# Attention columns of the first projection: six plain groups against three pairs of groups with two seven-product steps each

## The chip, the cores and the metric

The program runs on 1 core of one Trainium2 chip. The metric is the device time of one execution in microseconds (us), lower is better. The kernel before has a median of 1235.88 us over 3 runs (1235.82 to 1235.96).

The core has five engines with queues of their own: TensorE (PE, matmuls; its weight loads are listed apart as PEld), VectorE (DVE), ScalarE (ACT), GpSimd (POOL), and SyncE (SP), which here issues the loads from device memory. PE multiplies a moving operand by a stationary one and adds into PSUM, eight banks of 128 partitions by 512 fp32 columns; everything else lies in SBUF.

## What is computed

One decoder layer for 256 tokens and width 2048, in fp32, cut to what matters here:

```python
h = rms_norm(x, mix_norm_g[i])
z = h @ w_in[i]                                    # 2048 x 7184
mq, mk, mv, mo, mi, mf, fq, fk, fv, ff = jnp.split(z, split_points, axis=-1)
...                                                # mLSTM heads (A), forgetting attention (B) -> ha, hb
x = x + jnp.concatenate([ha, hb], axis=-1) @ w_out[i]
h = rms_norm(x, ffn_norm_g[i])
u = h @ w_up[i]
...                                                # causal conv, GELU, gate, w_down, and a gated last projection
```

The columns 4096 to 7183 of `w_in` (the gates mi, mf, ff and the attention inputs fq, fk, fv, 3088 columns) are the "FOX columns". They are computed first, then mq, mk, mv, mo.

## The kernel before

Weights arrive in fp32. Each weight block is split in two parts, hi (a cast to the PE's reduced fp32 form, on ACT) and lo (raw minus hi, on DVE); the left side is split in the same way once. One exact product then is three matmuls that add into one PSUM bank: left-hi by hi, left-hi by lo, left-lo by hi (lines 308, 309, 310 in this part of the program). The 256 tokens are two tiles of 128 rows (t = 0, 1); the inner dimension of 2048 is 16 K tiles of 128.

`token_group` (line 289) makes a group of n columns out of blocks. A block holds two K tiles of n columns (up to 1024 elements per partition), and takes 2 x 2 x 3 = 12 matmuls. The FOX columns are seven groups, of 512, 432 (five times) and 416 columns. In the first group x itself is also loaded, normed by a gain and transposed (lines 148, 149, 157) into `hT`, the left side. A group adds into two banks (one for each t) of the tag "mm", which has four; the tag "aux" has the other four, for transposes and for the side work. At a group's end ACT evacuates each bank, scaled by `rstd_mix` (line 751).

`run_stream` (line 250) runs all blocks of this part: the load of block i+3 is issued while block i is multiplied, into three load buffers (raw0 to raw2) in turn; up to three blocks are split ahead, into four pairs of buffers (hi0/lo0 to hi3/lo3), so a split waits until the block four back is multiplied. Between blocks it pulls two steps of the side work (head norms, gate arithmetic, attention heads, mLSTM heads), written as generators. A scheduler then sets the order on each engine's queue from its own estimate of when operands are there; the order in the source is its starting point.

Later, in the up projection, the kernel has the scheme that the change brings here: groups of four banks, with some pairs of K tiles done in seven products (lines 1336 to 1393). There 512 columns are a half, and the splits may run four units ahead.

Of the kernel before, what the change touches and what calls it, by code (L numbers as in the profile page):

```python
# [9 lines left out]
F32 = mybir.dt.float32  # L10
F32R = mybir.dt.float32r
AF = mybir.ActivationFunctionType
ALU = mybir.AluOpType
# [17 lines left out]
FOX_WIDTHS = (512, 432, 432, 432, 432, 432, 416)  # L31
# [8 lines left out]
AHEAD_DMA, AHEAD_SPLIT = 3, 3  # L40
# [14 lines left out]
def layer_kernel(  # L55
# [194 lines left out]
    def run_stream(blocks, pulls, ramp=False):  # L250

        nb = len(blocks)
        raws, parts = {}, {}
        split = 0
        for i in range(-AHEAD_DMA, nb):
            j = i + AHEAD_DMA
            if j < nb:
                src, _, _, load = blocks[j][:4]
                if load is not None:
                    load()  # L260
                kb, n = src.shape[1], src.shape[2]
                raws[j] = wp.tile([P, BLK], F32, tag=f"raw{j % RAW}", name=f"raw{j}", bufs=1)
                nc.sync.dma_start(out=raws[j][:, : kb * n].rearrange("p (k n) -> p k n", k=kb), in_=src)

            ahead = min(AHEAD_SPLIT, 1 + i // 2) if ramp else AHEAD_SPLIT
            while i >= -1 and split < min(nb, i + ahead + 1):
                j, split = split, split + 1
                src, _, prep, _ = blocks[j]
                if prep is not None:
                    prep()  # L270
                kb, n = src.shape[1], src.shape[2]
                w = kb * n
                raw = raws.pop(j)
                hi = wp.tile([P, BLK], F32R, tag=f"hi{j % PARTS}", name=f"hi{j}", bufs=1)
                lo = wp.tile([P, BLK], F32R, tag=f"lo{j % PARTS}", name=f"lo{j}", bufs=1)
                hi, lo = hi[:, :w], lo[:, :w]
                act.copy(hi, raw[:, :w])  # L277
                last["hi"] = traced()
                dve.tensor_sub(lo, raw[:, :w], f32(hi))  # L279
                parts[j] = [v.rearrange("p (k n) -> p k n", k=kb) for v in (hi, lo)]  # L280
            if i >= 0:
                blocks[i][1](*parts.pop(i))
                done[0] += 1
                pull(pulls)
# [4 lines left out]
    def token_group(w, korder, actT, c0, n, finish, tag="mm", prep=None, load=None):  # L289
# [7 lines left out]
        for bi, (k0, kb) in enumerate(starts):  # L297
            def fn(hi, lo, bi=bi, k0=k0):
                if bi == 0:
                    st["b"] = [bank(tag, f"tg{t}") for t in range(NT)]  # L300
                for t in range(NT):
# [9 lines left out]
                    if bi == len(starts) - 1:  # L311
                        finish(t, st["b"][t])
            pair = k0 % 2 == 0
            blocks.append((wsrc(w, k0, kb, c0, n), fn, pair and prep and (lambda k0=k0: prep(k0)) or None,
                           pair and load and (lambda k0=k0: load(k0)) or None))
        return blocks

# [29 lines left out]
    with mixers:  # L347
# [407 lines left out]
        ready_at = {"fq": (lambda: fox_norm("fq", 8),), "fk": (lambda: fox_norm("fk", 0),), "fv": (gate_math, fox_heads)}  # L755
        c0 = C_MI
        for n in FOX_WIDTHS:
            jobs = [j for name, o, w in runs_ if c0 < o + w <= c0 + n for j in ready_at[name]]
            kw = dict(prep=prep_x, load=load_x) if c0 == C_MI else {}
            add(c0, n, after(fox_evac(c0, n), *jobs), **kw)  # L760
            c0 += n
# [42 lines left out]
        for c in range(4):  # L804
            grp = token_group(w_out, kcat, lambda: catT, c * 512, 512, resid(c, ssq2, get_x2T, g_ffn))
            if c == 0:
                src, fn, _, _ = grp[4]
                grp[4] = (src, lambda hi, lo, fn=fn: (pull_all(), fn(hi, lo)), None, None)
            blocks.extend(grp)
        run_stream(blocks, 2, ramp=True)  # L810
# [3 lines left out]
    with tc.tile_pool(name="ffn", bufs=1) as fp:  # L814
# [44 lines left out]

        def sums_of(u, f, t):  # L860

            a11, a12 = u[:, 0, 0:P], u[:, 1, 0:P]
            dve.tensor_sub(f[:, 1::2], u[:, 0].rearrange("p (i c) -> p i c", c=P), u[:, :, P:S])
            dve.tensor_sub(f[:, 0], f[:, 3], a11)
# [170 lines left out]
        def units(blocks):  # L1035
            return [Unit([b[0]], b[1]) for b in blocks]
# [440 lines left out]
```

## Time and profile before

| what | value |
|---|---|
| median of 3 runs | 1235.88 us |
| the profiled execution: its time, its span | 1236.08 us, 1234.2 us |
| PE busy, PE weight loads busy | 1227.8 us (99%), 1035.5 us (84%) |
| DVE busy, ACT busy, POOL busy | 925.0 us (75%), 734.5 us (60%), 185.5 us (15%) |
| matmuls | 5620 |
| HBM read, mean rate | 247.46 MB, 208 GB/s |

The span runs from the first to the last instruction; 1.9 us of the profiled execution lie outside of it. Successive matmuls overlap in the profile (a row of 0.36 us can start every 0.19 us), so a matmul's price is the distance from one start to the next, not its listed duration. In a row of groups, the first number after the bar is the busy time in us, the second the mean duration in ns, and after the second bar stands the engine's idle time just before such instructions, with what ended it.

### The profile page before, as it was taken

What the parts mean: (1) busy time and instruction counts of PE and PEld (TensorE: products, weight loads), DVE (VectorE), ACT (ScalarE), POOL (GpSimd) and SP (SyncE); (2) the same over time, 40 slices, a digit from 0 to 9 for tenths busy, and PEclk for the clock granted to TensorE, in tenths of its full rate; (3) what the DMA queues carried; (4) which work ended last, traced back from release to release, by engine and by line L of the source; (5) the groups of instructions that cost most, each with busy time, mean ns of one, the idle gap of its engine ahead of it and who ended that gap; (6) DMA issues with size and microseconds to landing.
All of it is one profiled execution on the core that took longest, in us unless ns stands there. A gap on an engine that the chain in (4) does not pass through costs nothing.

```text
span 1234.2 us, 16266 instructions
## 1 busy us (share of the span) xinstructions
PE 1227.8 (99%) x5620; PEld 1035.5 (84%) x5620; DVE 925.0 (75%) x1107; ACT 734.5 (60%) x1071; POOL 185.5 (15%) x347
## 2 busy tenths in 40 slices
PE   9999999999999999999999999999999999999998
PEld 7999988888888888888888888888888888888887
DVE  6455566665565589789998898998788998898653
ACT  8565455554554465766676676757666555565542
POOL 2001256513304201011101100110110000050000
PEclk9999999999999999999999999999999999999999
DMA  8766878766567786777687678666897896777560
GB/s 257 195 187 185 226 222 219 208 196 179 171 188 218 222 307 207 242 220 235 211 271 243 184 253 271 223 180 213 245 315 245 305 332 210 258 231 257 176 214 35
DMA packets 139490, 276.35 MB, mean 224 GB/s; under 512 B 14905, under 2 KB 36913, under 8 KB 139281
## 3 DMA queue, kind: packets, MB, share of 16 engines
q1 hardware_dynamic: 127504, 256.87, 66.6%
q0 software_dynamic: 11520, 18.29, 5.2%
q8 instruction: 44, 0.72, 0.2%
q14 instruction: 37, 0.30, 0.1%
q10 hardware_dynamic: 385, 0.16, 0.0%
HBM read 247.46 MB, written 8.93 MB: 208 GB/s over the span
## 4 chain that ended last, share of the span: by engine, by line
PE 99%; DMA 0%; SPq 0%; DVE 0%; ACT 0%; issue 0%; DVEq 0%
PE tg L308 13%; PE tg L309 13%; PE tg L310 13%; PE up L1320 11%; PE up L1321 11%; PE up L1319 11%; PE dnP L1082 1%; PE upP L1319 1%; PE upP L1321 1%; PE upP L1320 1%; PE dnP L1080 1%; PE dnP L1081 1%; PE dn(0, 1)_7898 L1080 1%; PE dn(0, 0)_7894 L1080 1%; PE dn(1, 0)_7902 L1080 1%; PE dn(0, 1)_7898 L1082 1%
## 5 line engine op out<-in xcount | busy, mean ns | idle before, releaser
L279 DVE TENSOR_TENSOR lo<-raw,hi 128x1024 fp32r<-128x1024 f32 (+3 forms) x153 | 177.7, 1162 | 154.3 <-ACT hi L277 153.9
L277 ACT CAST hi<-raw 128x1024 fp32r<-128x1024 f32 (+3 forms) x153 | 153.4, 1003 | 155.3 <-PE tg L310 116.3
L1321 PE MATMUL up<-part,x2T 128*128 128x512 f32 x608 | 236.6, 389 | 0.0
L1320 PE MATMUL up<-part,x2T 128*128 128x512 f32 x608 | 236.5, 389 | 0.0
L1030 ACT CAST part<-raw 128x1024 fp32r<-128x1024 f32 (+1 forms) x147 | 147.1, 1009 | 112.4 <-PE up L1321 34.2
L1032 DVE TENSOR_TENSOR part<-raw,part 128x1024 fp32r<-128x1024 f32 (+1 forms) x141 | 163.2, 1162 | 34.3 <-ACT part L1030 31.7
L1319 PE MATMUL up<-part,x2T 128*128 128x512 f32 x608 | 185.0, 389 | 0.0
L309 PE MATMUL tg<-lo,hT 128*128 128x512 f32 (+2 forms) x480 | 181.5, 378 | 0.0
L308 PE MATMUL tg<-hi,hT 128*128 128x512 f32 (+2 forms) x480 | 180.8, 382 | 0.0
L310 PE MATMUL tg<-hi,hT 128*128 128x512 f32 (+2 forms) x480 | 180.3, 377 | 0.0
L1319 PEld LDWEIGHTS up<-part,x2T 128*128 128x128 f32 x608 | 114.1, 188 | 23.7
L1321 PEld LDWEIGHTS up<-part,x2T 128*128 128x128 f32 x608 | 114.1, 188 | 23.7
L1320 PEld LDWEIGHTS up<-part,x2T 128*128 128x128 f32 x608 | 114.1, 188 | 23.7
L310 PEld LDWEIGHTS tg<-hi,hT 128*128 128x128 f32 x480 | 90.1, 188 | 12.4
L309 PEld LDWEIGHTS tg<-lo,hT 128*128 128x128 f32 x480 | 90.2, 188 | 11.7 <-DVE lo L279 0.3
L308 PEld LDWEIGHTS tg<-hi,hT 128*128 128x128 f32 x480 | 89.7, 188 | 11.8
L195 POOL DMA_DIRECT2D EZ<-Y x66 | 35.1, 539 | 371.7 <-issue 205.1
L1030 ACT CAST part<-u36r 128x1024 fp32r<-128x1024 f32 (+1 forms) x46 | 47.9, 1043 | 33.5 <-PE up L1321 16.2
L1032 DVE TENSOR_TENSOR part<-u36r,part 128x1024 fp32r<-128x1024 f32 (+1 forms) x46 | 55.6, 1208 | 10.0 <-ACT part L1030 5.8
L1032 DVE TENSOR_TENSOR part<-u32r,part 128x1024 fp32r<-128x1024 f32 (+1 forms) x44 | 50.4, 1146 | 12.2 <-ACT part L1030 9.4
L1030 ACT CAST part<-u32r 128x1024 fp32r<-128x1024 f32 (+1 forms) x44 | 43.5, 994 | 21.1 <-PE up L1321 8.9
L310 PE MATMUL tg<-hi,catT 128*128 128x512 f32 x128 | 49.9, 390 | 0.0
(752 smaller groups left out, 2311.8 us busy)
## 6 DMA issues: line engine op xcount, KB each, us to landing
raw<-in_w_up_dram SPq DMA_DIRECT2D x78, 512.0 KB, 5.0
raw<-in_w_in_dram SPq DMA_DIRECT2D x71, 512.0 KB, 4.3
u36r<-in_w_up_dram SPq DMA_DIRECT2D x43, 512.0 KB, 5.0
raw<-in_w_down_dram SPq DMA_DIRECT2D x42, 512.0 KB, 5.9
u32r<-in_w_up_dram SPq DMA_DIRECT2D x34, 512.0 KB, 5.1
raw<-in_w_in_dram SPq DMA_DIRECT2D x40, 432.0 KB, 3.8
raw<-in_w_out_dram SPq DMA_DIRECT2D x32, 512.0 KB, 4.9
xs<-in_w_up_dram SPq DMA_DIRECT2D x21, 512.0 KB, 4.8
```

Of the source, the lines that this page charges most:

```text
L195: (other if other and (4 * a + b) % 3 else pool).dma_start(out=c[32 * b : 32 * b + 32, a::4], in_=y[32 * a : 32 * a + 32, :, b])
L277: act.copy(hi, raw[:, :w])
L279: dve.tensor_sub(lo, raw[:, :w], f32(hi))
L308: pe.matmul(o, ah, hi[:, i, :], start=first, stop=False)
L309: pe.matmul(o, ah, lo[:, i, :], start=False, stop=False)
L310: pe.matmul(o, al, hi[:, i, :], start=False, stop=last)
L1030: act.copy(r32(hi), raw)
L1032: dve.tensor_sub(r32(lo), raw, hi)
L1080: pe.matmul(o, ah, hi, start=first, stop=False)
L1319: pe.matmul(o, ah, hi, start=start, stop=False)
L1320: pe.matmul(o, ah, lo, start=False, stop=False)
L1321: pe.matmul(o, al, hi, start=False, stop=stop)
```

## The change

The FOX columns become one plain group of 512 and three pairs of groups. A pair holds two halves of 430 columns (428 in the last pair) side by side; a block is one K tile of both halves, and the pair adds into four banks, (t, half). Twelve of its 16 K tiles ("p") are plain: 2 x 2 x 3 = 12 matmuls. K tiles 0, 1 ("a") and 2, 3 ("b") are each a 2 x 2 block product (two token tiles, two K tiles, two halves) done by seven products of three matmuls, 21 in place of 24, in four units of 3, 6, 6 and 6 matmuls. Three of the seven add straight into the pair's banks, four go into four banks of their own (P1, P5, P6, P7), shared by a and b. The order of units in a pair is `"pppp" "apapapap" "bpbpbpb" "p"`; the two sets of four banks, "mm" and "aux", change roles from pair to pair, so all eight banks are used.

For the sums of left parts (`make_S`, `sums_of`) DVE and ACT make two tiles S_h in the first group. For the sums of weights DVE adds halves of the loaded tiles (lines 414, 415, 425, 426), and 4 x (430 + 3 x 860) columns are split for a and b where 2 x 2 x 864 were. When b is done, ACT and DVE make four combined results out of the P banks in unused space of `spare` (lines 436 to 440), and at the pair's end DVE adds them, scaled, to the evacuated outputs (line 941).

Loading changes for the whole stream: the oldest free buffer is taken as soon as there is one, and from the third unit of the first pair to the end of the last, four more buffers (`more`, in the space of the second tiles of tags aT1 and aT2, which the attention output takes later) stand beside raw0 to raw2. Number of products, widths and evacuation of the other columns stay; from the output projection (w_out) on, the orders of all engines are the same as before.

```diff
-FOX_WIDTHS = (512, 432, 432, 432, 432, 432, 416)
+FOX_FIRST, FOX_HALVES = 512, (430, 430, 428)
+FOX_ORDER = "pppp" "apapapap" "bpbpbpb" "p"
...
+        def free(j):
+            tags = [t for t in [*raw_tags, *more] if t not in held and (t in raw_tags or more[t][0] <= j < more[t][1])]
+            return sorted(tags, key=lambda t: used.get(t, -1))
...
+        def part(hi, lo, raw):
+            act.copy(hi, raw)
+            last["hi"] = traced()
+            dve.tensor_sub(lo, raw, f32(hi))
...
+            while True:
+                if loaded < nb and (i >= -1 or loaded <= i + RAW) and len(free(loaded)) >= len(blocks[loaded].srcs):
+                    put(loaded)
+                    loaded += 1
+                elif i >= -1 and split < min(nb, i + ahead + 1, loaded):
...
+    def pair_group(w, actT, c0, n, order, tags, S_of, z_, evac, added):
...
+        def plain(k):
+            def fn(hi, lo):
+                if k == first:
+                    st.update({(t, h): bank(tags[0], f"pg{t}{h}") for t in range(NT) for h in range(2)})
+                for t in range(NT):
+                    for h in range(2):
+                        o = st[t, h]
+                        three(o[:, :n], *left(k, t), half(hi[:, 0], h), half(lo[:, 0], h), k == first, k == KD - 1)
+                        if k == KD - 1:
+                            evac(t, h, o)
...
+            def fn1(hi, lo):
+                sum_of(1, left(2 * r, 0), half(hi, 0), half(lo, 0))
...
+            def fn2(hi, lo):
+                three(st[0, 0][:, :n], *left(2 * r + 1, 0), half(hi, 0), half(lo, 0))
+                three(st[0, 1][:, :n], *S(4), half(hi, 1), half(lo, 1))
...
+            def split3(part, hi, lo):
+                ra, rb_ = one.raws
+                dve.tensor_add(half(ra, 0), half(ra, 1), half(ra, 0))
+                dve.tensor_add(half(ra, 1), half(rb_, 1), half(ra, 1))
+                part(hi[:, : 2 * n], lo[:, : 2 * n], ra[:, : 2 * n])
+                return ()
+
+            def fn3(hi, lo):
+                sum_of(5, S(1), half(hi, 0), half(lo, 0))
+                sum_of(7, S(3), half(hi, 1), half(lo, 1))
...
+            def fn4(hi, lo):
+                sum_of(6, S(2), half(hi, 1), half(lo, 1))
+                three(st[1, 0][:, :n], *left(2 * r + 1, 1), half(hi, 0), half(lo, 0))
...
+                act.copy(z[0], st[1][:, :n])
+                dve.tensor_add(z[1], st[6][:, :n], z[0])
+                dve.tensor_add(z[2], st[7][:, :n], z[1])
+                for i in (1, 3):
+                    dve.tensor_sub(z[i], st[5][:, :n], z[i // 2 + 1])
...
+        def make_S(r):
+            d = mp.tile([P, 512], F32, tag="qk", name="Sd", bufs=2).rearrange("p (k c) -> p k c", c=256)
+            f = sm.tile([P, 512], F32, tag="junk", name="Sf").rearrange("p (i c) -> p i c", i=4)
+            h = hT[:, 2 * r : 2 * r + 2, :]
+            dve.tensor_add(d, f32(h[..., 0:256]), f32(h[..., 256:512]))
+            S_h[r] = mp.tile([P, 4, 256], F32R, tag=("sq", "col")[r], name=f"S_h{r}")
+            sums_of(d, f, S_h[r])
...
+                            dve.scalar_tensor_tensor(out=v, in0=z_fox[2 * t + h][:, l:r], scalar=r1["t"][:, t : t + 1],
+                                                     in1=v, op0=ALU.mult, op1=ALU.add)
...
+        more = {f"m{i}{k}": (at + 2, until, lambda i=i, k=k: second(i)()[:, k]) for i in (1, 2) for k in range(2)}
```

Three places show what the scheduler makes of it. The first is the start of the program. On DVE, before, the split of the third block (`lo_198`) follows the four low parts of the first transposed tiles:

```order
L149 SCALAR_TENSOR_TENSOR hT_138<-xT_158,g_mix,hT_138 128x256
L149 SCALAR_TENSOR_TENSOR hT_138<-xT_163,g_mix,hT_138 128x256
L149 SCALAR_TENSOR_TENSOR hT_138<-xT_187,g_mix,hT_138 128x256
L149 SCALAR_TENSOR_TENSOR hT_138<-xT_192,g_mix,hT_138 128x256
L279 TENSOR_TENSOR lo_198<-raw_153,hi_197 128x1024
```

Of the change, at the same place (Sd is the sum of the hi and lo parts of two K tiles of hT, once for a and once for b):

```order
L150 SCALAR_TENSOR_TENSOR hT_138<-xT_155,g_mix,hT_138 128x256
L150 SCALAR_TENSOR_TENSOR hT_138<-xT_160,g_mix,hT_138 128x256
L150 SCALAR_TENSOR_TENSOR hT_138<-xT_187,g_mix,hT_138 128x256
L150 SCALAR_TENSOR_TENSOR hT_138<-xT_192,g_mix,hT_138 128x256
L912 TENSOR_TENSOR Sd<-hT_138 128x512 x2
L287 TENSOR_TENSOR lo_198<-raw_153,hi_197 128x1024
```

Two additions now stand ahead of that split. On SP, before, the loads of the first group's last blocks (512 wide) are followed by those of the next group:

```order
L263 DMA raw_208<-in_w_in_dram 128x2x512
L263 DMA raw_259<-in_w_in_dram 128x2x512
L263 DMA raw_292<-in_w_in_dram 128x2x512
L263 DMA raw_343<-in_w_in_dram 128x2x512
L263 DMA raw_389<-in_w_in_dram 128x2x432
L263 DMA raw_407<-in_w_in_dram 128x2x432
```

Of the change, the same loads, with four into the new buffers (more_337, more_340: the third and fourth plain unit of the first pair, and the two tiles of its a) among them:

```order
L276 DMA raw_202<-in_w_in_dram 128x2x512
L276 DMA more_337<-in_w_in_dram 128x860
L276 DMA raw_229<-in_w_in_dram 128x2x512
L276 DMA more_337<-in_w_in_dram 128x860
L276 DMA raw_250<-in_w_in_dram 128x2x512
L276 DMA raw_283<-in_w_in_dram 128x2x512
L276 DMA more_340<-in_w_in_dram 128x860 x2
L276 DMA raw_315<-in_w_in_dram 128x860
L276 DMA raw_335<-in_w_in_dram 128x860
```

The pair's first two units (raw_315, raw_335) now come behind four loads of later units. The second place is PE where the first group ends. Before, the first matmuls of the next group (tg_455, tg_456, in two unused banks) even start inside the last block (hi_373):

```order
L308 MATMUL tg_176<-hi_373,hT_140 128x512
L308 MATMUL tg_177<-hi_373,hT_140 128x512
L308 MATMUL tg_455<-hi_391,hT_138 128x432
L308 MATMUL tg_456<-hi_391,hT_138 128x432
L309 MATMUL tg_176<-lo_374,hT_140 128x512
```

Of the change, from the fifth matmul of the pair on (pg_482 to pg_485 are the pair's four banks; pg_484 and pg_485 lie in those of tg_179 and tg_180, the first group's, which ACT has to evacuate first):

```order
L353 MATMUL pg_483<-lo_402,hT_138 128x430
L354 MATMUL pg_483<-hi_401,hT_138 128x430
L352 MATMUL pg_482<-hi_419,hT_138 128x430
L352 MATMUL pg_483<-hi_419,hT_138 128x430
L353 MATMUL pg_482<-lo_420,hT_138 128x430
L354 MATMUL pg_482<-hi_419,hT_138 128x430
L353 MATMUL pg_483<-lo_420,hT_138 128x430
L354 MATMUL pg_483<-hi_419,hT_138 128x430
L352 MATMUL pg_482<-hi_449,hT_138 128x430
L352 MATMUL pg_483<-hi_449,hT_138 128x430
L352 MATMUL pg_484<-hi_401,hT_138 128x430
L353 MATMUL pg_484<-lo_402,hT_138 128x430
```

With the four before these rows, fourteen matmuls into the first two banks (six of the first unit, six of the second, two of the third) stand ahead of the first into the third bank, and twenty-one ahead of the first into the fourth. The third place is PE in the first pair. Before, every block is four products of three:

```order
L308 MATMUL tg_455<-hi_430,hT_138 128x432
L309 MATMUL tg_455<-lo_431,hT_138 128x432
L310 MATMUL tg_455<-hi_430,hT_138 128x432
L308 MATMUL tg_455<-hi_430,hT_138 128x432
L309 MATMUL tg_455<-lo_431,hT_138 128x432
L310 MATMUL tg_455<-hi_430,hT_138 128x432
```

Of the change, the second unit of a (hi_533, two products) and the start of the plain unit behind it (hi_549, all four banks) and of the third unit of a (hi_559):

```order
L352 MATMUL pg_482<-hi_533,hT_138 128x430
L352 MATMUL pg_483<-hi_533,S_h_472 128x430
L353 MATMUL pg_482<-lo_534,hT_138 128x430
L354 MATMUL pg_482<-hi_533,hT_138 128x430
L353 MATMUL pg_483<-lo_534,S_h_472 128x430
L354 MATMUL pg_483<-hi_533,S_h_472 128x430
L352 MATMUL pg_482<-hi_549,hT_139 128x430
L352 MATMUL pg_483<-hi_549,hT_139 128x430
L352 MATMUL pg_484<-hi_549,hT_139 128x430
L352 MATMUL pg_485<-hi_549,hT_139 128x430
L352 MATMUL pgP_614<-hi_559,S_h_472 128x430
L352 MATMUL pgP_618<-hi_559,S_h_472 128x430
```

A unit of a brings six matmuls where a plain one brings twelve, on weights that need the same cast and subtraction.

190 lines of the change are left out of this document (140 added, 50 removed).

## The prediction

> **What bounds the kernel now.** I read the page first, for which engine is never idle and what the chain that ended last consists of.
>
> ```profile
> span 1234.2 us, 16266 instructions
> PE 1227.8 (99%) x5620; PEld 1035.5 (84%) x5620; DVE 925.0 (75%) x1107; ACT 734.5 (60%) x1071; POOL 185.5 (15%) x347
> ...
> PE   9999999999999999999999999999999999999998
> PEld 7999988888888888888888888888888888888887
> DVE  6455566665565589789998898998788998898653
> ...
> PE 99%; DMA 0%; SPq 0%; DVE 0%; ACT 0%; issue 0%; DVEq 0%
> ```
>
> TensorE is busy in every slice and is 99% of the chain. But listed matmuls overlap, so I asked next for PE's waits:
>
> ```profile
> PE warm L98 <- DVE ones L94: 1.1, 1, 1.1
> PE xT L157 <- DMA xs<-in_x_dram: 1.1, 1, 1.1
> ```
>
> Those two, at the very start, are all. So time is gained only by fewer or shorter matmuls, and lost as soon as one waits. What one costs I took from windows inside the FOX columns (34 to 124 us: all 432 wide; 126 to 143: all 416 wide) and, for comparison, from the up projection (460 to 540: 512 wide, with seven-product units):
>
> ```profile
> core 0: us, PE busy (x) PEld busy (x) DVE busy (x) ACT busy (x) POOL busy (x), PEclk, DMA share, GB/s
> 34.00:124.00 90.00, 90.00 (x467) 87.24 (x466) 47.03 (x49) 50.76 (x113) 7.54 (x6) 1.00 0.69 188
> 126.00:143.00 17.00, 17.00 (x91) 16.83 (x91) 8.70 (x11) 8.38 (x10) 4.82 (x10) 1.00 0.85 234
> ...
> 460.00:540.00 80.00, 80.00 (x355) 66.24 (x354) 66.93 (x67) 50.77 (x66) 6.37 (x12) 1.00 0.69 212
> ```
>
> The counts include the one or two that a window's edges cut, so I take one and a half off: 90 / 465.5 = 193 ns for 432 columns, 17 / 89.5 = 190 ns for 416, 80 / 353.5 = 226 ns for 512. From 512 to 432 the price falls by 33 ns, from 432 to 416 by 3 only: in the FOX columns the weight load is nearly continuous (87.24 of 90 us), so it begins to be the floor. For 428 to 430 columns I take 193 ns, the 432 price. The clock is 1.00 in all three.
>
> **The change, part by part.**
>
> *Fewer matmuls.* Before, six groups of 16 K tiles, two token tiles and three matmuls: 6 x 16 x 2 x 3 = 576. After, each pair has 12 plain units of 12 and two sevens of 21: 144 + 42 = 186, so 558 in all. 18 are gone, at 193 ns: -3.5 us. The columns are the same 2576 in total, so width adds nothing. Weight loads fall with the matmuls.
>
> The Trainium skill (TensorE: Matmul & The Clock Gate, Back-to-back issue gap) gives 131 ns for a sustained 512-column matmul paired with its weight load, and 81 ns for 128; between the two, a 430-column one would be worth about 120 ns by estimate, and the 18 some 2.2 us. The trace's 226 ns for 512 disagrees with it, and the trace decides; I give this outcome (1234.1 us) no chance of its own.
>
> *Work added off PE.* Groups of DVE over the whole program give additions, additions out of PSUM, and scaled additions:
>
> ```profile
> L895 DVE SCALAR_TENSOR_TENSOR EZ<-xs,rstd_ffn,EZ 128x1024 f32<-128x1024 f32 x22 | 27.9, 1280 | 0.0
> ...
> L1383 DVE TENSOR_TENSOR xs<-upP,xs 128x512 f32<-128x512 f32 x11 | 7.6, 687 | 1.1 <-PE upP L1321 0.7
> ...
> L1360 DVE TENSOR_TENSOR raw<-raw 128x512 f32<-128x512 f32 x7 | 4.8, 688 | 0.1
> ```
>
> Groups of the window 34 to 124 give the plain splits and a head norm's multiplication:
>
> ```profile
> L279 DVE TENSOR_TENSOR lo<-raw,hi 128x864 fp32r<-128x864 f32 x37 | 39.1, 1057 | 40.0 <-ACT hi L277 40.0
> L277 ACT CAST hi<-raw 128x864 fp32r<-128x864 f32 x37 | 33.8, 915 | 32.8 <-PE tg L310 30.7 <-DMA raw<-in_w_in_dram 2.1
> ...
> L434 DVE TENSOR_TENSOR fq<-fq,r_fq 128x1024 f32<-128x1024 f32 x2 | 2.4, 1223 | 1.0 <-POOL r_fq L170 1.0
> ```
>
> DVE costs about 1.05 ns a column here (1057 - 688 over 352), so 430 columns are 0.60 us. A seven adds 0.60 + 3 x 1.06 - 2 x 1.06 = 1.7 us of subtractions and 4 x 0.60 = 2.4 us of additions; a pair adds four results out of PSUM (2.4) and the scaled additions, 860 columns for each t in four to six pieces (about 2.9). That is 13.5 us a pair. DVE stood at 47.03 of 90 us (52%); with 40 us more in some 107 it comes to about 90%. ACT gains about 1.4 us a seven and 0.5 a pair, 56% to about 66%. I cost both at nothing, and this cover is thinner than any other: it is PE's own time. Evidence for it: in the window at 460, DVE is 84% busy, in whole slices of the page it is 90% or more, and PE waits for neither. The tightest stretch is "apapapap" of the second and third pair: 69 matmuls (13.3 us) against DVE's 0.60 + 7 x 1.06 + 2.4 = 10.4 us, plus the two 1.22 us multiplications of a head norm, 12.9. If four split buffers cannot bridge that, it costs up to 2.4 us in each of two pairs; from the UP window I take 0. What would be late next is a plain unit's lo, and PE behind it.
>
> *The two sums Sd.* They stand on DVE ahead of lo_198. The timeline before (start, duration, engine):
>
> ```profile
> 9.53 1.23 DVE L279 TENSOR_TENSOR lo<-raw,hi 128x1024 fp32r<-128x1024 f32 x1 [0.39 <-ACT hi L277]
> ...
> 11.04 0.60 PE L157 MATMUL xT<-ident,xs 128*128 128x128 f32 x4
> 11.06 1.78 DVE L149 SCALAR_TENSOR_TENSOR hT<-xT,g_mix,hT 128x256 fp32r<-128x256 f32 x4 [0.31 <-ACT hT L148]
> ...
> 11.39 0.47 PE L309 MATMUL tg<-lo,hT 128*128 128x512 f32 x1
> ```
>
> DVE is free at 9.14 (9.53 less its idle 0.39). Two additions of 0.69 put lo's start at about 10.5 in place of 9.53 and its end at 11.7 in place of 10.76; PE wants it at 11.39. Cost 0.3 us at that matmul; the next split had waited longer for ACT than the delay, so it is not passed on. Bounds 0 and 0.4; I take 0.2, since PE later in this group makes up some of it.
>
> *Four loads ahead.* Each is 128 x 860 x 4 = 440 KB, 1.76 MB together, ahead of the pair's own first two. Windows of the first transfers (the last two columns are the DMA engines' busy share and GB/s):
>
> ```profile
> 16.00:18.00 2.00, 2.00 (x12) 1.62 (x11) 1.91 (x3) 2.00 (x9) 0.00 (x0) 1.00 1.01 322
> 18.00:20.00 2.00, 2.00 (x10) 1.65 (x9) 1.56 (x3) 2.00 (x7) 0.00 (x0) 1.00 0.82 216
> 20.00:22.00 2.00, 2.00 (x13) 1.70 (x13) 1.51 (x3) 2.00 (x5) 0.00 (x0) 1.00 0.60 130
> 22.00:24.00 2.00, 2.00 (x11) 1.38 (x9) 1.83 (x4) 1.95 (x7) 0.00 (x0) 1.00 0.85 250
> 24.00:26.00 2.00, 2.00 (x10) 1.65 (x10) 1.91 (x5) 1.42 (x3) 0.00 (x0) 1.00 0.86 238
> ```
>
> The timeline of ACT (the next group's first two casts, then the first group's evacuation) and of PE at the handover:
>
> ```profile
> 26.20 0.92 ACT L277 CAST hi<-raw 128x864 fp32r<-128x864 f32 x1 [0.78 <-DMA raw<-in_w_in_dram]
> ...
> 27.98 0.91 ACT L277 CAST hi<-raw 128x864 fp32r<-128x864 f32 x1
> ...
> 32.01 0.69 ACT L751 ACTIVATE fq<-tg,rstd_mix 128x512 f32<-128x512 f32 x1 [0.74 <-PE tg L310]
> ```
>
> ```profile
> 32.66 0.39 PE L310 MATMUL tg<-hi,hT 128*128 128x512 f32 x1
> 32.89 0.35 PE L309 MATMUL tg<-lo,hT 128*128 128x432 f32 x1
> ```
>
> At the saturated 322 GB/s the four take 5.5 us; the idle shares from 18 to 26 us are worth (0.18 + 0.40 + 0.15 + 0.14) x 2 = 1.7 us, and I allow 0.3 until 28. So the pair's first load lands up to 3.5 us later: its cast would go from 26.20 to 29.7, its lo (cast 0.92, subtraction 1.06) end at 31.7, against PE's first use at 32.9. The second goes from 27.98 to 31.5, its lo ends at 33.5 against 32.9 + 8 x 0.193 = 34.4. Cost 0, with 0.9 us to spare. With none of the idle time usable it would be 1.1 us late. Bounds 0 and 1.1; a gain is excluded, PE waits for no load there today.
>
> *The third and fourth bank.* ACT evacuates the first group's banks behind three casts and the S_h cast; before, it did so at 32.01. If the second cast starts at 31.5 and ends at 32.4, the S_h cast (512 wide, like an evacuation 0.69), the third cast (0.92) and two evacuations (0.69 each) follow, and the banks are free at about 34.7 and 35.4. PE reaches them at 32.9 + 14 x 0.193 = 35.6 and 32.9 + 21 x 0.193 = 37.0. Cost 0, bound 0.5. At the later handovers the new banks are the P banks, emptied early by ACT and DVE, and fourteen or more matmuls stand between; at the last, four evacuations stand ahead of the 512-wide mq group. I take 0.2 us for all handovers together.
>
> *Loading rule, head work, the rest.* SP issues 48 loads of the pairs where it issued 48 of the groups, POOL no more than before. Same order from w_out on: 0. The gather of the first head columns on POOL begins later, because one of its buffers holds S_h and DVE's transposes are later. The heads' matmuls so move up to 90 matmuls later among the mq and mk columns and meet their old places before the mLSTM heads; plain products stand around them, so 0.
>
> Sum: -3.5 + 0.2 + 0.2 = -3.1 us on the profiled execution's own 1236.08, which is 0.2 above the median; on the median's scale 1235.88 - 3.1 = 1232.8 us.
>
> **Rivals.** What a measurement of this kernel can tell from no change I put at 0.2%, 2.5 us.
>
> *Handovers and tight stretches eat the gain* (no measurable change). Loads late by 1.1, banks by 0.5, and one of the two DVE stretches by 1 to 2 us give back 1 to 3.5 us: 1233.4 to 1235.9. For it: PE's order has rows that reach into three units to fill time, so little is spare. Against it: each sum above ends with something to spare.
>
> *The sevens pace PE* (slower). A seven's unit is a serial chain on two engines, additions 1.2, cast 0.92, subtraction 1.06, 3.2 us, and its buffer comes free only four units earlier, that is 2 x 12 + 6 matmuls or 5.8 us before its use. If queues on DVE at 90% add more than the 2.6 us left, each of 24 units waits. At 0.14 us a unit the gain is gone, from 0.24 us a unit the kernel is over 0.2% slower; at 0.4 us it is 1242 us. Against it: the same chain at 512 columns runs in the up projection without a wait, though there four units ahead.
>
> *Unaligned halves slow the matmuls* (slower). The second half now starts 1720 bytes into a tile, not 1728. The trace's nearest rows are 257-column and 256-column products, the first at offsets of 1032 bytes:
>
> ```profile
> L671 PE MATMUL mob<-mv,WT 128*128 128x257 f32 x24 | 6.0, 380 | 0.0
> L579 PE MATMUL ob<-PT,fv 128*128 128x256 f32 x16 | 4.8, 379 | 0.0
> ```
>
> 380 against 379 ns shows no penalty, though in another number format. The price would be 0.56 us for each ns; from 6 ns the gain is gone, from 11 ns it is over 0.2% slower (1238.5 us). The Trainium skill (SBUF — State Buffer, Door 1: The DMA port swizzle) says that SBUF has 16-byte lines and that each crossing to a new line costs; a start in the middle of a line adds one line to 108, which by estimate is under 2 ns, and no run here shows it.
>
> *The 416 price* (faster still). If 430 columns run at the 190 ns of the 416 window, 558 x 3 ns = 1.7 us more is gained: 1231.1 us.
>
> **How the numbers follow.** The forecast, 0.55; its own range is 1232.2 to 1233.4. The 416 price, 0.07. Handovers eat the gain, 0.25. The sevens pace PE, 0.08; unaligned halves, 0.05. So faster 0.62, same 0.25, slower 0.13. The range takes in the forecast, most of the 416 price and the handovers: 1231.2 to 1236.0.
>
> **What the profile after would show.** 5602 matmuls; PE's waits still two rows of 1.1 us, with nothing for lo or pg; 430-column windows at 193 ns; DVE at 80 to 90% between 33 and 140 us; PE's first 512-wide mq matmul about 3 us earlier than before. Wrong would be: a PE wait at L352 or L353 for lo or hi (the sevens), for ACT fq (banks), for a load near 33 us, or a distance between matmuls well off 193 ns where PE does not wait.

## The result, and the profile after

| | before | changed |
|---|---|---|
| median | 1236.32 us (22 runs) | 1234.08 us (22 runs, 1233.56 to 1236.12) |
| ratio | | 0.998, 95% interval 0.9974 to 0.9987 |
| profiled execution: its time, its span | 1236.08, 1234.2 us | 1233.69, 1232.0 us |

The changed kernel is 2.2 us faster; the forecast was 3.1. The interval of the ratio, 1.6 to 3.2 us, still takes in 3.1, so it is the traces and not the times that say which term of the forecast was off. The changed kernel's page, its first lines and DVE's row of slices:

```profile
span 1232.0 us, 16329 instructions
...
PE 1226.3 (100%) x5602; PEld 1032.9 (84%) x5602; DVE 962.2 (78%) x1181; ACT 743.4 (60%) x1088; POOL 186.7 (15%) x347
...
DVE  6788857665565689888998898998788998898553
```

The 18 matmuls are gone, and DVE has 37 us more to do: its slices 2 to 5 (31 to 154 us) read 7888 where they read 4555. PE's waits, all of them:

```profile
PE warm L99 <- DVE ones L95: 1.1, 1, 1.1
PE xT L158 <- DMA xs<-in_x_dram: 0.4, 1, 0.4
```

No wait for a split, a bank or a load of the FOX columns. So the missing 0.9 us is not a wait; what is left is the matmuls' own pace. The windows of before and after, over the same 70 us and (after) the last pair; columns as in the prediction:

```profile
34.00:104.00 70.00, 70.00 (x364) 67.83 (x363) 35.25 (x36) 38.72 (x81) 2.91 (x1) 1.00 0.71 192
```

```profile
34.00:104.00 70.00, 70.00 (x360) 67.36 (x359) 55.34 (x72) 43.51 (x85) 3.72 (x1) 1.00 0.62 194
106.00:140.00 34.00, 34.00 (x176) 32.87 (x176) 29.35 (x43) 23.20 (x52) 4.18 (x2) 1.00 0.49 149
```

PE never rests in either, and yet fewer matmuls of 430 columns fit into 70 us (360) than of 432 (364). With one and a half off for the edges, as in the prediction: 193.1 ns before, 195.3 after. From the start times of all narrow matmuls of each trace, the distance from one start to the next comes to:

```
                 columns  count  mean ns     narrow part
before           432      480    193.6
                 416       96    189.2       111.10 us
after            430      372    195.6
                 428      186    194.4       108.92 us
```

The narrow part lost 2.18 us and the span 2.19. The rest cancels out: the wait for x is 0.7 us shorter, which the change does not explain (over all profiles of this record, whatever the kernel, it is 0.3 to 1.8 us), the first 512-wide matmul starts only 0.2 us earlier, and from there to the end of the FOX columns the work outside the narrow part takes 25.38 us where it took 25.21. Behind the FOX columns nothing moved: the first mq matmul starts 2.2 us earlier (141.40 in place of 143.60), the first of the up projection too (429.32 in place of 431.54).

### The profile page after: what moved, and what is told of

Read it like the earlier page. It is cut to its first block, busy times and chain, and to the rows that moved or that the text cites. A ratio compares the mean times of both kernels' runs of the same rounds, so it can differ in the third digit from the quotient of the medians.

```text
span 1232.0 us, 16329 instructions
## 1 busy us (share of the span) xinstructions
PE 1226.3 (100%) x5602; PEld 1032.9 (84%) x5602; DVE 962.2 (78%) x1181; ACT 743.4 (60%) x1088; POOL 186.7 (15%) x347
## 4 chain that ended last, share of the span: by engine, by line
PE 99%; DMA 0%; SPq 0%; DVE 0%; ACT 0%; issue 0%; DVEq 0%
PE up L352 11%; PE up L354 11%; PE up L353 11%; PE tg L341 10%; PE tg L342 10%; PE tg L343 10%; PE pg L352 3%; PE pg L353 3%; PE pg L354 3%; PE dnP L1270 1%; PE dnP L1269 1%; PE upP L354 1%; PE upP L353 1%; PE upP L352 1%; PE dnP L1268 1%; PE dn(0, 1)_7989 L1270 1%
## 5 line engine op out<-in xcount | busy, mean ns | idle before, releaser
L287 DVE TENSOR_TENSOR lo<-raw,hi 128x1024 fp32r<-128x1024 f32 (+3 forms) x130 | 153.2, 1181 | 108.1 <-ACT hi L285 107.8
L353 PE MATMUL up<-part,x2T 128*128 128x512 f32 x608 | 236.5, 389 | 0.0
L285 ACT CAST hi<-raw 128x1024 fp32r<-128x1024 f32 (+3 forms) x130 | 132.3, 1017 | 123.4 <-PE tg L343 69.6
L352 PE MATMUL up<-part,x2T 128*128 128x512 f32 x608 | 185.0, 389 | 0.0
L353 PEld LDWEIGHTS up<-part,x2T 128*128 128x128 f32 x608 | 114.1, 188 | 23.7
L352 PEld LDWEIGHTS up<-part,x2T 128*128 128x128 f32 x608 | 114.1, 188 | 23.6
L343 PE MATMUL tg<-hi,hT 128*128 128x512 f32 x288 | 113.6, 395 | 0.0
L342 PE MATMUL tg<-lo,hT 128*128 128x512 f32 x288 | 113.2, 393 | 0.0
L341 PE MATMUL tg<-hi,hT 128*128 128x512 f32 x288 | 112.5, 397 | 0.0
L1218 ACT CAST part<-u36r 128x1024 fp32r<-128x1024 f32 (+1 forms) x46 | 47.8, 1041 | 34.7 <-PE up L354 16.3
L342 PEld LDWEIGHTS tg<-lo,hT 128*128 128x128 f32 x288 | 54.1, 188 | 11.1 <-DVE lo L287 0.2
L343 PEld LDWEIGHTS tg<-hi,hT 128*128 128x128 f32 x288 | 54.1, 188 | 11.1
L341 PEld LDWEIGHTS tg<-hi,hT 128*128 128x128 f32 x288 | 53.8, 188 | 10.6
L353 PE MATMUL pg<-lo,hT 128*128 128x430 f32 (+1 forms) x156 | 55.7, 357 | 0.0
```

The lines of the kernel that those rows point to most:

```text
L285: act.copy(hi, raw)
L287: dve.tensor_sub(lo, raw, f32(hi))
L341: pe.matmul(o, ah, hi[:, i, :], start=first, stop=False)
L342: pe.matmul(o, ah, lo[:, i, :], start=False, stop=False)
L343: pe.matmul(o, al, hi[:, i, :], start=False, stop=last)
L352: pe.matmul(o, ah, hi, start=start, stop=False)
```

## The experiments

The open question: why does a narrow matmul take 195.2 ns on average now, and 192.9 (111.10 / 576) before, with no wait in either? The theories as the expectations name them. W: the new widths, in form W1 the start of the second half off a multiple of 16 bytes, in form W2 the width itself. D: DVE's heavier load shares memory with PE. O: the new order on PE. A unit before ran three products of one bank after another; a unit now mostly runs its four hi products first and the others afterwards. F: the load of the weights sets a floor, and it costs more near it. G: only widths off a multiple of 32 columns cost more.

All verdicts rest on the distances and on the narrow part (the sum of the distances), from one profile each. The times beside them carry other things too. The part behind the FOX columns differs by up to 1.6 us among these profiles, in part by waits of the up projection, as this one of the third experiment:

```profile
PE upP L352 <- ACT part L1209: 0.3, 1, 0.3
```

The start of the program differs as well. The windows from 8 to 12 us of the changed kernel and of the first experiment, where the listed clock is 0.61:

```profile
8.00:12.00 4.00, 4.00 (x23) 3.17 (x22) 3.97 (x8) 3.61 (x10) 0.18 (x1) 1.00 1.06 330
```

```profile
8.00:12.00 4.00, 4.00 (x13) 3.16 (x12) 3.97 (x8) 2.73 (x8) 0.16 (x1) 0.61 1.05 326
```

In six of the fourteen profiles (the first and the seventh to eleventh experiment) this window holds 13 to 15 matmuls, in the other eight 23 or 24; three of the six list a clock of 0.57 to 0.64 there, three list 1.00. In the six, the stretch from the first 512-wide matmul to the first mq matmul takes 26.0 to 26.6 us outside the narrow part, in the others 25.0 to 25.7. So a difference of 1 or 2 us between two of the times below says little by itself. In all windows over narrow matmuls that are shown here the clock is 1.00.

**First: the changed kernel with aligned halves.**

```diff
-FOX_FIRST, FOX_HALVES = 512, (430, 430, 428)
+FOX_FIRST, FOX_HALVES = 512, (432, 432, 424)
```

> The changed kernel with halves of 432, 432 and 424 columns in place of 430, 430 and 428: the same products, but each second half starts at a multiple of 16 bytes (1728 and 1696). In the changed kernel the mean distance between the starts of narrow matmuls is 195.6 ns at 430 columns and 194.4 at 428; before it was 193.6 at 432 and 189.2 at 416. Theory W (width or start of the halves): 432 goes back to 193.6 and 424 to about 191.5, so 372 x 193.6 + 186 x 191.5 = 107.6 us in place of 108.9, and the time falls by 1.3 us to about 1232.8. Theory D (DVE, busy for 80% of these windows in place of 53%, shares the memory that PE reads) and theory O (the new order, over four banks and with sums as weights): the distances stay near 196 at 432 and 193 at 424, and the time stays within 0.4 us of the changed kernel's 1234.1.

Measured: 432 at 196.4 ns, 424 at 192.6; narrow part 108.88 us, as in the changed kernel; 1234.35 us (10 runs). Its window:

```profile
34.00:104.00 70.00, 70.00 (x358) 66.94 (x357) 55.12 (x74) 43.36 (x85) 3.71 (x1) 1.00 0.64 195
```

The same 432 columns that cost 193.6 before cost 2.8 ns more here. So aligned starts alone do not bring the old price back in the changed kernel.

**Second: the kernel before with the new widths.**

```diff
-FOX_WIDTHS = (512, 432, 432, 432, 432, 432, 416)
+FOX_WIDTHS = (512, 430, 430, 430, 430, 428, 428)
```

> The kernel before with its FOX groups 430, 430, 430, 430, 428 and 428 wide in place of five of 432 and one of 416: the old order, the old load on DVE, 576 narrow matmuls, only the widths and the start of each second K tile (1720 and 1712 bytes) as in the changed kernel. Theory W: distances of 195.6 and 194.4 ns, so 384 x 195.6 + 192 x 194.4 = 112.4 us in place of 111.1, and a time 1.3 us above the kernel before. Theories D and O: 193 at 430 and 192.5 at 428, 111.1 us, the same time as the kernel before.

Measured: 195.6 and 195.9 ns, narrow part 112.73, 1238.0 us: 1.6 us slower than before, by the new widths and the starts that come with them, without sevens, four banks or more work on DVE.

```profile
34.00:104.00 70.00, 70.00 (x359) 67.30 (x358) 34.77 (x36) 38.69 (x82) 2.91 (x1) 1.00 0.71 191
```

**Third: the pairs without the sevens** (their order is then `"pppp"` four times, `make_S` and the additions of `added` fall away).

```diff
-FOX_ORDER = "pppp" "apapapap" "bpbpbpb" "p"
+FOX_ORDER = "pppp" "pppp" "pppp" "pppp"
...
-        for r in range(2):
-            with_after(blocks[at - 1 - r], lambda r=r: make_S(r))
```

> The changed kernel without its sevens: 16 plain units in each pair of groups, 576 narrow matmuls, four banks and the same halves and load buffers, no additions on DVE. Theory W: distances of 195.6 and 194.4 ns, 112.5 us in the narrow groups, about 1.3 us slower than the kernel before: 1237.5. Theory O (the order over four banks): the same distances. Theory D: 193 and 192.5 ns, since DVE has the old load, so 111.1 us and the time of the kernel before, 1236.3. With 18 matmuls less at 195.2 the changed kernel would by W and O have won 3.5 us against this one, by D 2.2.

Measured: 195.6 and 193.8 ns, narrow part 112.34, 1239.28 us. Against this kernel the sevens take away 112.34 - 108.92 = 3.4 us, 18 times 190 ns: the term -3.5 of the prediction is there in full. What the change paid is in the other 558. On the order it says less than its expectation has it: without the sevens the scheduler mostly went back to the order of before. At 430 columns 112 of 127 hi products (L352) are followed by their lo product (L353), in the changed kernel 47 of 124. So this kernel has four banks and the shifted start in nearly the old order, and stands at the 195.6 ns of the second experiment: four banks add nothing at 430.

**Fourth: the kernel before with a busier DVE.**

```diff
+        def busy():
+            dve.tensor_add(spare[:, 2048:2480], spare[:, 2560:2992], spare[:, 3072:3504])
...
+            if c0 != C_MI:
+                blocks[at:] = [(s_, lambda hi, lo, fn=fn: (fn(hi, lo), busy()), p_, l_) for s_, fn, p_, l_ in blocks[at:]]
```

> The kernel before with one more addition on DVE after each of the 48 units of the narrow groups (432 columns of a scratch tile, read and written by nothing else): DVE goes from 53% to about 80% of these windows, the share that it has in the changed kernel; everything that PE does is as before. Theory D: the distance at 432 goes from 193.6 to about 196 and at 416 from 189.2 to about 191.5, the time up by 1.3 us. Theories W and O: 193.6 and 189.2, the time of the kernel before.

Measured: 193.8 and 189.2 ns, narrow part 111.19, 1236.72 us, ratio 1.0004 (0.9994 to 1.0013).

```profile
34.00:104.00 70.00, 70.00 (x363) 67.73 (x362) 54.95 (x74) 40.26 (x85) 2.91 (x1) 1.00 0.73 195
```

DVE has the changed kernel's load (54.95 against 55.34 of 70 us) and PE keeps its pace. D falls.

**Fifth and sixth: the start of the second K tile, each way.** In the fifth, 430 and 428 columns with the second tile 432 columns on; in the sixth, 432 and 416 columns with it two columns further.

```diff
-                nc.sync.dma_start(out=raws[j][:, : kb * n].rearrange("p (k n) -> p k n", k=kb), in_=src)
+                m = 432 if n < 512 else n
+                nc.sync.dma_start(out=raws[j][:, : kb * m].rearrange("p (k m) -> p k m", k=kb)[:, :, :n], in_=src)
```

> The kernel before with groups of 430 and 428 columns as in the second experiment, but the second K tile of a unit starts at 1728 bytes (432 columns on) in place of 1720 and 1712. Theory W1 (it is the start off a multiple of 16 bytes that costs): back to 193 ns at 430 and 192 at 428, 111.0 us of narrow matmuls, 1.7 us faster than the second experiment. Theory W2 (it is the width itself): 195.6 and 195.9 ns as in the second experiment, 112.7 us.

> The kernel before with its own widths of 432 and 416, but the second K tile of a unit starts two columns further on, at 1736 and 1672 bytes, which are no multiples of 16. Theory W1: about 195.5 ns at 432 and 191 at 416, 1.1 us slower than before. Theory W2: 193.6 and 189.2, as before.

Measured, fifth: 193.4 ns at 430, 195.5 at 428, narrow part 111.79, 1237.06 us. Sixth: 196.7 at 432, 190.0 at 416, 112.65, 1237.93 us. The windows of the fifth and of the sixth:

```profile
34.00:104.00 70.00, 70.00 (x364) 67.97 (x363) 35.41 (x36) 38.47 (x81) 2.91 (x1) 1.00 0.71 191
```

```profile
34.00:104.00 70.00, 70.00 (x358) 67.00 (x357) 34.89 (x36) 38.25 (x81) 2.91 (x1) 1.00 0.70 190
```

At 430 and 432, in this order, the start does it, both ways: 364 matmuls when the second tile starts at 1728 bytes, 358 or 359 when not. My expectation of the fifth had a slip: 1712 bytes, the start at 428 columns, is a multiple of 16 already, so W1 had nothing to say there; and 428 stayed dear wherever its second tile began.

**Seventh: the order alone.** The kernel before, own widths and starts, with each narrow unit's four hi products first.

```diff
+                    for t, i, ah, al in ops:
+                        pe.matmul(st["b"][t][:, :n], ah, hi[:, i, :], start=bi == 0 and i == 0, stop=False)
+                    for t, i, ah, al in ops:
...
+                        pe.matmul(o[:, :n], ah, lo[:, i, :], start=False, stop=False)
+                        pe.matmul(o[:, :n], al, hi[:, i, :], start=False, stop=last)
```

> The kernel before with its own widths and starts, but each unit of the narrow groups issues its four products of the hi weights and the hi tile first and then the four pairs of the other two, which is the order that the changed kernel's units have on PE. Theory O (with aligned halves it is the order that took 432 columns from 193.6 to 196.4 ns): 196.4 ns at 432, 1.3 us slower than before. If it is not the order: 193.6, and the price of the first experiment lies in the sevens, or in four banks in place of two.

Measured: 196.6 ns at 432, 188.9 at 416, narrow part 112.52, 1238.17 us.

```profile
34.00:104.00 70.00, 70.00 (x357) 66.83 (x356) 34.09 (x37) 39.28 (x84) 2.91 (x1) 1.00 0.71 190
```

So a shifted start (second and sixth) and another order (seventh) each end at 195.6 to 196.7 ns. They do not add up: the changed kernel has both and stands at 195.6. That looks less like two costs than like one low price that either of them loses.

Nor does the low price belong to one of the three products. In the kernel before, the matmul behind one of line 308, 309 or 310 starts 196.8, 193.6 or 190.4 ns after it; with the start shifted (sixth) the same three are 197.8, 196.1 and 196.2. At 430 columns they are 190.2, 196.7 and 193.2 with the start at 1728 (fifth), and 195.0, 194.8 and 197.0 at 1720 (second). At 432 most of the gain is behind line 310, at 430 behind 308 and 310.

**Eighth: widths well apart, in the new order.**

```diff
+FOX_FIRST, FOX_HALVES = 512, (416, 416, 456)
```

> The changed kernel with halves of 416, 416 and 456 columns. From 512 columns at 226.7 ns and 432 at 193.6 a column is worth 0.41 ns; the load of a matmul's weights takes 187.6 ns whatever the width. Theory F (where the columns' time comes down to within some 5 ns of the load of the weights, the two alternate as the longer one and their unevenness adds 2 to 3 ns; on either side of that stretch it does not): 416 at 189 to 190.5 and 456 at 203.5 ns, 372 x 190 + 186 x 203.5 = 108.5 us, 0.4 us faster than the changed kernel. Theory O alone (2 to 3 ns added by the new order at any width under 512): 192 and 206, 109.7 us, 0.8 us slower than the changed kernel.

Measured: 416 at 189.2, 456 at 206.9 ns, narrow part 108.87, 1234.66 us. F is wrong at 456, which is far from the load of the weights and 3.4 ns dearer than F had it; O alone is wrong at 416, which is 2.8 ns cheaper than O had it, and nearly right at 456.

**Ninth: the changed kernel with 432, in sequence.** The changed kernel with halves of 432, 432 and 424, and each narrow matmul issued after the one before it in the code.

```diff
+                    if "mm" in last:
+                        order.enter_context(tc.issue_after(last["mm"]))
+                    pe.matmul(o, a, m, start=start and i == 0, stop=stop and i == 2)
+                last["mm"] = traced()
```

> The changed kernel with halves of 432, 432 and 424 columns (starts at multiples of 16 bytes) and with the order of its narrow matmuls fixed as the code issues them: hi, lo and the low weights' product of one bank, then those of the next. The kernel before mostly ran so. If the start of the halves and the order are the whole of the excess: 193.6 ns at 432 and 190.5 at 424, 372 x 193.6 + 186 x 190.5 = 107.4 us in place of 108.9, and 1232.6 us. If four banks or the sums as weights cost of themselves: 196 and 192.5, 108.8 us, 1234.1. If lo now comes late, since a bank's second product follows its first at once, there are waits for DVE lo at these matmuls and the time is above 1234.

Measured: 194.8 ns at 432 and 192.8 at 424, without two short stalls at the changes from pair to pair, together 0.7 us; with them 109.01 us, and 1234.31 us (11 runs). One stall, in PE's timeline:

```profile
72.07 0.35 PE L363 MATMUL pg<-lo,hT 128*128 128x432 f32 x1
72.26 0.90 PE L363 MATMUL pg<-hi,hT 128*128 128x432 f32 x2
73.00 0.36 PE L363 MATMUL pg<-lo,hT 128*128 128x432 f32 x1
```

DVE's timeline beside it:

```profile
71.53 1.11 DVE L448 TENSOR_TENSOR spare<-pgP,spare 128x432 f32<-128x432 f32 x2
```

The next but one matmul after 72.26 starts 0.74 us on, where 0.39 is usual. DVE ends its reading of a P bank, which the next pair adds into, at 72.64, and the second of the two matmuls starts at 72.70; at the other handover it is 109.19 and 109.25. So these are most likely waits for a bank, though the profile lists none. None of the three outcomes of the expectation came as it stands. The order of before brings back more than half of the 2.8 ns, and costs as much at the handovers, which the changed kernel's own order had covered.

**Tenth and eleventh: the same three widths in the new order and in the old.**

```diff
+FOX_FIRST, FOX_HALVES = 512, (448, 416, 424)
...
+FOX_WIDTHS = (512, 448, 448, 416, 416, 424, 424)
```

> The changed kernel, in its own order, with halves of 448, 416 and 424 columns: all starts at multiples of 16 bytes, 448 and 416 also of 128. Between 416 at 189.3 and 512 at 226.7 ns, which no order has moved so far, a straight line gives 201.7 at 448; by 0.41 ns a column from 512 it is 200.2. Theory G (only widths off a multiple of 32 columns have the excess): 448 at 200 to 202, so 186 x (200.2 + 189.3 + 192.5) = 108.3 us, 0.6 us faster than the changed kernel. Theory O (the order costs 3 ns at every width between 416 and 512, as it did at 432 and 456): 203.3, 108.8 us, the same time as the changed kernel.

> The kernel before, in its own order, with groups of 448, 448, 416, 416, 424 and 424 columns: the widths of the tenth experiment in the old order, all starts at multiples of 16 bytes. Theory O (the order costs about 3 ns at every width from 424 to 456, and nothing at 416): 448 at 200.2 ns (0.41 a column above 432 at 193.6), 416 at 189.2, 424 at 190.3, 192 x (200.2 + 189.2 + 190.3) = 111.3 us, the time of the kernel before. If these widths cost what they cost in any order and 432 in the old order was the exception: 202.6, 189.3 and 192.4 ns, 112.2 us, 1.1 us slower than before.

Measured in the new order: 202.6, 189.3 and 192.8 ns, 108.76 us, 1233.92 us (11 runs). In the old order: 202.7, 187.8 and 193.3 ns, 112.07 us, 1238.23 us. Their windows over the 448 columns, new order first:

```profile
36.00:70.00 34.00, 34.00 (x170) 31.51 (x169) 24.38 (x29) 18.15 (x27) 0.00 (x0) 1.00 0.63 190
```

```profile
34.00:70.00 36.00, 36.00 (x179) 33.27 (x178) 16.13 (x17) 18.70 (x33) 0.00 (x0) 1.00 0.71 191
```

34 / 168.5 = 201.8 and 36 / 177.5 = 202.8 ns. These widths cost the same in both orders, so O falls as a general price of the order, and G with it, since 448 is a multiple of 32. The second outcome that the eleventh expectation names is what came: 432 columns in the old order were the exception.

**Twelfth: the width of the rest of the kernel.**

```diff
+FOX_FIRST, FOX_HALVES = 512, (512, 388, 388)
```

> The changed kernel, in its own order, with halves of 512, 388 and 388 columns. Theory O, with the excess at every width above the load of the weights: 512 at about 230 ns, 186 x 230 + 372 x 188.5 = 112.9 us. If the excess is gone at 512, as in the up projection, which runs in the same order: 226.7 ns, 112.3 us. 388 columns in both cases at the 188 to 189 ns of 416, the load of the weights and little more. Either way 3.4 to 4 us slower than the changed kernel.

Measured: 512 at 227.7 ns, 388 at 176.2 (without the wait named next), and 1234.08 us, the changed kernel's time. One wait is new, the 0.6 us of the first mq matmul for the last evacuation. The window over the 388 columns, and the loads of their weights in it:

```profile
76.00:106.00 30.00, 30.00 (x173) 30.00 (x172) 25.63 (x37) 21.64 (x56) 3.56 (x1) 1.00 0.61 183
```

```profile
L354 PEld LDWEIGHTS pg<-hi,hT 128*128 128x128 f32 x48 | 9.0, 188 | 0.0
...
L352 PEld LDWEIGHTS pg<-hi,hT 128*128 128x128 f32 x47 | 8.5, 188 | 0.0
```

```profile
PE tg L341 <- ACT fv L934: 0.6, 1, 0.6
```

The loads are listed with 188 ns as everywhere, yet matmuls start every 176 ns: successive loads overlap, and their listed duration is no floor. That was the premise of my 3.4 us.

**Together.** The distances in the kernels with pairs in their own order, from 388 to 456 columns, lie within 0.7 ns of a straight line through the first and the last, 176.2 and 0.451 for each column above 388 (30.7 ns over 68 columns). All of them against it, in ns:

```
columns  line   pairs                           plain groups, as before
388      176.2  176.2
416      188.8  189.2, 189.3                    189.2, 187.8, 188.9; start shifted 190.0
424      192.4  192.6, 192.8; sequence 192.8    193.3
428      194.3  194.4; no sevens 193.8          195.9, 195.5
430      195.2  195.6; no sevens 195.6          195.6; start at 1728: 193.4
432      196.1  196.4; sequence 194.8           193.6; start shifted 196.7; hi first 196.6
448      203.3  202.6                           202.7
456      206.9  206.9
512      232.1  227.7
```

Pairs of the same width in their own order agree within 0.2 ns. The plain groups do so less: 416 columns with the same order and starts stand at 189.2 and 187.8 in two kernels, so something that no run here varied moves them by 1.4. The 3 ns at 432 show in two kernels on the low side (193.6, 193.8) and in three on the high side (196.4, 196.6, 196.7).

The narrow parts sort the same way: 112.1 to 112.7 us with 576 matmuls (second, third, sixth, seventh, eleventh), 108.6 to 109.0 with 558 (the changed kernel, first, eighth, tenth, and with their stalls the ninth and the twelfth). Between the two lie 18 matmuls of 195 ns, 3.5 us. Only the kernel before (111.1), the same with a busier DVE (111.2) and in part the fifth (111.8) run under that level. The change won its 3.5 us and gave up the 1.3 us by which the kernel before ran under the usual price. Why 430 or 432 columns with the second tile at 1728 bytes, in that one order, run 1.8 to 2.5 ns under the line stays open, as does why 512 lies 4 to 5 ns under it. None of the versions tried is measurably faster than the changed kernel.

## Why the prediction was right and wrong

- **Fewer matmuls, -3.5 us.** The count was right (5602), and the third experiment gives 3.4 us for it. The failed step is the price: "for 428 to 430 columns I take 193 ns, the 432 price". Measured 195.6 and 194.4; over 558 matmuls, against the mean of 192.9 before, +1.3 us. This one term is more than the whole miss of 0.9 us. The mechanism, fewer matmuls on a PE that never waits, held; the time lies outside the forecast's own 1232.2 to 1233.4 and inside the whole range.
- **The reading behind that step** was that the weight load "begins to be the floor" between 432 and 416. The 176 ns at 388 columns refute it. The kernel before has a row that does so too, the 256-column matmuls of the last projection, with the same three products. PE's and the weight loads' timelines:

```profile
1220.35 0.28 PE L1275 MATMUL tl<-part,x3T 128*128 128x256 f32 x1
1220.47 0.28 PE L1276 MATMUL tl<-part,x3T 128*128 128x256 f32 x1
```

```profile
1220.36 0.19 PEld L1276 LDWEIGHTS tl<-part,x3T 128*128 128x128 f32 x1
1220.48 0.19 PEld L1277 LDWEIGHTS tl<-part,x3T 128*128 128x128 f32 x1
```

  They start every 119 ns on average, each with a load of its own, listed with 0.19 us. The rows quoted in the prediction could have warned: a straight line from 416 (190) to 512 (226) gives 195 at 430. The 432 window lay below the line through its neighbours, and I took the exception for the rule.
- **The sums Sd, +0.2 us.** DVE's timeline of the changed kernel:

```profile
8.90 1.29 DVE L912 TENSOR_TENSOR Sd<-hT 128x512 f32<-128x512 f32 x2
10.11 1.22 DVE L287 TENSOR_TENSOR lo<-raw,hi 128x1024 fp32r<-128x1024 f32 x1
```

  That lo ends at 11.33, not at 11.7, and 0.57 us later than before. The work from the first 512-wide matmul to the end of the FOX columns, narrow part aside, grew by 0.17 us; no run singles out this delay as its cause, and among the eight profiles with 23 or 24 matmuls from 8 to 12 us the same stretch differs by up to 0.7 us.
- **Four loads ahead, 0.** Right. ACT's and PE's timelines at the handover:

```profile
28.59 1.90 ACT L285 CAST hi<-raw 128x860 fp32r<-128x860 f32 x2
...
31.72 0.68 ACT L891 ACTIVATE fq<-tg,rstd_mix 128x512 f32<-128x512 f32 x1
32.68 0.69 ACT L891 ACTIVATE fq<-tg,rstd_mix 128x512 f32<-128x512 f32 x1 [0.28 <-PE tg L343]
```

```profile
32.48 0.55 PE L352 MATMUL pg<-hi,hT 128*128 128x430 f32 x2
32.87 0.36 PE L353 MATMUL pg<-lo,hT 128*128 128x430 f32 x1
```

  The first cast starts at 28.6 where I had 29.7, the second ends at 30.5 where I had 32.4. The expected delay was too long, not too short.
- **Banks and handovers, +0.2 us.** Measured 0: the first group's banks are free at 32.4 and 33.4, not at 34.7 and 35.4, and no later handover shows a wait. The ninth experiment shows the 0.7 us that two handovers cost in another order, and the twelfth 0.6 us at the last handover with narrower halves.
- **DVE at nothing.** Right: 79% (55.34 of 70) and 86% (29.35 of 34), no PE wait, and the fourth experiment shows that the load itself does not slow PE. A and b of a pair together split 2 x (430 + 3 x 860) columns, not 4 x as the description of the change has it; the prediction's 1.7 us a seven is worked out from the right number.
- **The rivals.** Handovers that eat the gain: the time came out within that rival's 1233.4 to 1235.9, by luck, since not one of its mechanisms is in the trace. Sevens that pace PE: no wait at L352 or L353. The 416 price: not at 430. Unaligned halves: in the changed kernel they cost nothing (430 stands 0.4 ns above the line, the aligned 432 of the first experiment 0.3). The Trainium skill (SBUF — State Buffer, Door 1: The DMA port swizzle), which charges each crossing to a new 16-byte line, does not tell these cases apart. In the old order the shifted start costs 3.1 ns at 432, but 428 with its start at a multiple of 16 is as dear as 430 without. And 430 columns touch 108 lines from byte 1720 as from 1728, so the one line more of the prediction is not there, yet the two starts differ by 2.2 ns (195.6 and 193.4).
- **The outcome without a chance.** The estimate from the Trainium skill (TensorE: Matmul & The Clock Gate, Back-to-back issue gap) gave 1234.1 us, which is the measured time, but on the scale of the earlier median: as a gain it is 1.8 us, and 2.2 were measured. Its matmul of 120 ns is not what ran: the trace has 195 ns, and the near agreement is luck: it comes from a loss of 1.3 us that this estimate does not contain.

## What to carry to other kernels

Before a price per instruction is carried to a neighbouring shape, lay it beside two other shapes of the same kernel: a row that lies off the line through its neighbours may hold for its exact width, start and order alone. When a tuned kernel's inner loop is given a new shape, allow for the small luck of the old one being lost, as it was here, and price all instructions that stay, not only those that go. A listed duration of an overlapped instruction, such as a weight load, is not a floor until a narrower case shows that it is; such a case may already stand elsewhere in the same trace.

## What was not expected of the hardware

Between 388 and 456 columns a matmul of these types costs 0.45 ns a column in the steady stream and about 1 ns beside it (176.2 - 388 x 0.451), and 512 columns cost 4 to 5 ns less than that line says; 256 columns in the last projection (119 ns) cost 3 ns more. Weight loads listed with 188 ns follow each other every 176 ns at 388 columns, and every 120 at 256. And the pace of a stream without a single wait can move by 3 ns of 194 with the order of the same matmuls (193.6 to 196.6) or with eight bytes in the start of their operand (193.6 to 196.7), while DVE busy for 78% of the time in place of 50% moved it by 0.2.
